# Two-layer SSD, GLA and block attention trunk: nine weight pieces split by a rounding and an adding load, mixer steps kept apart, one copy moved to ScalarE

## The chip, the cores and the metric

One core of a Trainium2 chip runs the whole program. The metric is device time in microseconds of one execution, the median of three.

## The reference, cut to what matters

A sequence of 256 tokens with 1024 channels goes through two layers and a last norm, all in float32.

```python
h = rms_norm(x, norm_w); u = h @ w_in            # first layer, w_in is 1024 x 5408
z_a, xbc, dt_raw, q_b, k_b, v_b, gate_lr, g_b = split_cols(u, EVEN_SPLITS)
y_a = rms_norm(ssd_chunked_scan(...) * silu(z_a), ssd_norm_w)          # after conv and silu of xbc
o_b = rms_norm(gla_chunked(q_b, k_b, v_b, log_decay), gla_norm_w) * silu(g_b)
x = x + concatenate([y_a, o_b]) @ w_out
h = rms_norm(x, norm_w); q, k, v, z = split(h @ w_in2)                 # second layer
x = x + (moba_attention(q, k, v) * silu(z)) @ w_out2                   # causal, one block of 256
return rms_norm(x, final_norm)
```

## The kernel before, in words

Every weight product is done in three matmuls of a rounded format (float32r): a number is split into a high part, which is its rounding, and a low part, which is what the rounding left, and `mm3` adds high by high, high by low and low by high. The weights arrive as pieces: `fetch` loads one of 128 x 1024 floats (512 KB) from SyncE's queue into one of 4 raw buffers, and `split` makes the high part on ScalarE (line 77) and the low part on VectorE (line 78), each into one of NW = 7 buffers. `plan` lists the pieces in the order of use, and `need` asks for the next few ahead of it (`prefetch`, AHEAD = 4), so that loads and splits stand in the queues before the matmuls that use them.

The first layer runs block by block in the order ORDER_A: a number j is a block of 128 columns (24 matmuls of 128 x 256, accumulated in `pb`), "a2" to "a4" are groups of 416 columns (48 matmuls, `pa`). Blocks 18 to 25 are the gate z. Then come the output products `pc1` (the GLA half) and `pc0` (the SSD half), the second layer's `pv`, `pp` and the last product `pf`.

Between those matmuls TensorE does the mixers' own small work: the SSD scan (`co_pair`: transposes `xtp`, decays `ab`, products `yp`), the GLA (`co_gla_pair`: scores `gs`, outputs `go`, transposes `obt`), the turns of `x1` into `h1` (`co_turn`: transposes `htp`, named by the token half and the column half, as `htp11`) and a few more. Each is a Python generator; every `yield` gives a delay in nanoseconds, a step is due when a planner's clock, which adds a cost for each matmul, has passed it, and `mm3` calls `due()` behind every three matmuls. All steps that are due then go out at once. TensorE's order is as written; the other engines are ordered by a scheduler when the program is built. Each engine works through its queue in order.

`part` runs one half of the tokens (tt) over eight k-blocks of three matmuls. `pv01` is the second half of the tokens in the second layer's first product: its k-blocks 4 to 7 read what `htp11` turned, rounded by ScalarE (line 741) with the low part made by VectorE (line 742).

In `co_gla_pair` the scores of two heads are copied from PSUM by ScalarE (line 604), masked by GpSimd (line 605), and a crossing block of 64 x 128 is copied over by VectorE (line 607). For each head then come two squares on ScalarE, two small VectorE steps (lines 623, 624), a power on GpSimd (line 625), one more VectorE step and the scaled output `ob`.

Of the kernel before, what the change touches and what calls it, by code (L numbers as in the profile page):

```python
# [19 lines left out]
EPS = 1e-6  # L20
# [25 lines left out]
def trunk(ctx, tc, xw_d, x_d, cst_d, mat_d, gw2_d, fn_d, wa_d, wb_d, wc_d, wv_d, wp_d, wf_d, out_d):  # L46
    nc = tc.nc
    V, S, G, TE = nc.vector, nc.scalar, nc.gpsimd, nc.tensor

    cpool = ctx.enter_context(tc.tile_pool(name="consts", bufs=1))  # L50
    wraw = ctx.enter_context(tc.tile_pool(name="wraw", bufs=4))
    whi = ctx.enter_context(tc.tile_pool(name="whi", bufs=NW))
    wlo = ctx.enter_context(tc.tile_pool(name="wlo", bufs=NW))
    big = ctx.enter_context(tc.tile_pool(name="big", bufs=1))
    tmp = ctx.enter_context(tc.tile_pool(name="tmp", bufs=2))
    sm = ctx.enter_context(tc.tile_pool(name="sm", bufs=2))
# [8 lines left out]
    def pm(name):  # L65
        return psm.tile([P, 512], F32, name=name, tag="m")


    def fetch(src, kbs, cols, name):
        raw = wraw.tile([P, kbs, cols], F32, name="r_" + name, tag="raw")  # L70
        nc.sync.dma_start(raw, src)
        return raw

    def split(raw, kbs, cols, name):
        hi = whi.tile([P, kbs, cols], F32R, name="h_" + name, tag="hi")
        lo = wlo.tile([P, kbs, cols], F32R, name="l_" + name, tag="lo")
        S.activation(hi, raw, AF.Copy)  # L77
        V.tensor_sub(lo, raw, hi.bitcast(F32))  # L78
        return hi, lo

    pieces, index, got, raws = [], {}, [], []

    def plan(key, src, kbs, cols):
        index[key] = len(pieces)
        pieces.append((key, src, kbs, cols))

    def prefetch(end):
        for j in range(len(got), min(len(pieces), end)):
            k_, src, kbs, cols = pieces[j]
            name = "_".join(str(q_) for q_ in k_)  # L90
            if j >= len(raws):
                raws.append(fetch(src, kbs, cols, name))
            got.append(split(raws[j], kbs, cols, name))
# [10 lines left out]
    for kb in range(KB):  # L104
        for c in range(2 if kb < 2 else 1):
            plan(("a01", kb, c), None, 1 if kb < 2 else 2, 416)
    for j in ORDER_A:
        if isinstance(j, str):
# [17 lines left out]

    clock = {"now": 0.0, "seq": 0}
    waiting = []  # L130

    def spend(ns):
# [2 lines left out]
    def spawn(gen, delay=0.0):  # L135
        clock["seq"] += 1
        heapq.heappush(waiting, (clock["now"] + delay, clock["seq"], gen))

    def step():
        _, _, gen = heapq.heappop(waiting)  # L140
        try:
            spawn(gen, next(gen))
        except StopIteration:
            pass

    def due():
        while waiting and waiting[0][0] <= clock["now"]:
            step()

    def drain():  # L150
        while waiting:
            clock["now"] = max(clock["now"], waiting[0][0])
            step()
# [8 lines left out]
    def tr(out, in_):  # L162
        TE.transpose(out, in_, ident)
        spend(107)
# [43 lines left out]
    tri = [mat[:, M_TRI + P * i:M_TRI + P * i + P] for i in range(2)]  # L208
    mask = mat[:, M_MASK:M_MASK + 3 * P]
    ones = cpool.tile([P, 1], F32, name="ones")  # L210
    mhalf = cpool.tile([P, 2], F32, name="mhalf")
    V.memset(ones, 1.0)
    V.memset(mhalf, -0.5)
    scanm = big.tile([P, 16, 64], F32, name="scanm", tag="s3")
# [9 lines left out]
    with tc.manual_schedule(engines={mybir.EngineType.DVE, mybir.EngineType.Activation}):  # L224
        for kb in range(KB):
# [3 lines left out]
            else:  # L229
                S.activation(hhi[:, kb, :], xk, AF.Copy, scale=en)  # L230
            V.scalar_tensor_tensor(hlo[:, kb, :], xk, en, hhi[:, kb, :].bitcast(F32),
                                   op0=ALU.mult, op1=ALU.subtract)
# [30 lines left out]
    rhalf, rsq, rsv, rsh = (cpool.tile([P, 2], F32, name=n_) for n_ in ("rhalf", "rsq", "rsv", "rsh"))  # L263
# [320 lines left out]
    def co_gla_pair(b):  # L584
        e1, e2, e3, e4, dl = env["gla"]
        qs, ks = env["qs"], env["ks"]
        rows = [slice(64 * j, 64 * j + 64) for j in range(2)]
        heads = [2 * b, 2 * b + 1]
        sps = [pm(f"gs{h}") for h in heads]
        blkv = lambda a, r, c0, n: a[r, 4 * b + c0:4 * b + c0 + n, :].rearrange("p a b -> p (a b)")  # L590
        for sp_, r in zip(sps, rows):
            mm(sp_[:, 0:P], blkv(e2, r, 0, 2), blkv(e1, r, 0, 2))
        for sp_, r in zip(sps, rows):
            mm(sp_[:, P:2 * P], ks[r, b, :, :].rearrange("p a b -> p (a b)"),
               qs[r, b, :, :].rearrange("p a b -> p (a b)"))
        for sp_, r in zip(sps, rows):
            mm(sp_[:, 2 * P:3 * P], blkv(e2, r, 2, 2), blkv(e1, r, 2, 2))
        for i in range(2):
            for sp_, r in zip(sps, rows):
                mm(sp_[0:64, 384 + 64 * i:448 + 64 * i], e4[r, 4 * b + 2 * i, :], e3[r, 4 * b + 2 * i + 1, :])  # L600
        sTs = []
        for h, sp_ in zip(heads, sps):
            sT = tmp.tile([P, 3, P], F32, name=f"sT{h}", tag="t1d")
            S.activation(sT.rearrange("p a b -> p (a b)"), sp_[:, 0:3 * P], AF.Copy)
            G.affine_select(out=sT[:, 0:3:2, :], in_=sT[:, 0:3:2, :], pattern=[[0, 2], [1, P]],
                            compare_op=ALU.is_ge, fill=0.0, base=0, channel_multiplier=-1)
            V.tensor_copy(sT[0:64, 0:3:2, 64:P], sp_[0:64, 384:512].rearrange("p (a b) -> p a b", a=2))
            sTs.append(sT)
        yield DL["gla1"]
        obs = []  # L610
        for h, sT in zip(heads, sTs):
            op = pm(f"go{h}")
            vc = slice(P * h, P * h + P)
            mm(op[:, 0:P], sT[:, 0, :], v[:, 0, vc])
            mm(op[:, P:T], sT[:, 1, :], v[:, 0, vc], True, False)
            mm(op[:, P:T], sT[:, 2, :], v[:, 1, vc], False, True)
            sq = tmp.tile([P, T], F32, name=f"osq{h}", tag="t1e")
            ss = sm.tile([P, 2], F32, name=f"oss{h}", tag="oss")
            for tt in range(2):
                S.activation(sq[:, tt * P:tt * P + P], op[:, tt * P:tt * P + P], AF.Square,  # L620
                             accum_out=ss[:, tt:tt + 1])
            rr = sm.tile([P, 2], F32, name=f"rr{h}", tag="rr")
            V.tensor_tensor(ss, ss, rsv, op=ALU.mult)
            V.tensor_scalar(ss, ss, EPS, None, op0=ALU.add)
            G.tensor_tensor(rr, ss, mhalf, op=ALU.pow)  # L625
            V.tensor_tensor(rr, rr, rsh, op=ALU.mult)
            ob = tmp.tile([P, T], F32, name=f"ob{h}", tag="t1f")
            for tt in range(2):
                V.scalar_tensor_tensor(ob[:, tt * P:tt * P + P], op[:, tt * P:tt * P + P], rr[:, tt:tt + 1],
                                       gs[:, tt, vc], op0=ALU.mult, op1=ALU.mult)  # L630
            obs.append(ob)
        yield DL["gla2"]
        obhi, oblo = env["ob"]
        gn = cst[:, C_GN:C_GN + 1]
        for h, ob in zip(heads, obs):
            tp = pm(f"obt{h}")
            for tt in range(2):
                tr(tp[:, tt * P:tt * P + P], ob[:, tt * P:tt * P + P])
            S.activation(obhi[:, h, :], tp[:, 0:T], AF.Copy, scale=gn)
            V.scalar_tensor_tensor(oblo[:, h, :], tp[:, 0:T], gn, obhi[:, h, :].bitcast(F32),  # L640
                                   op0=ALU.mult, op1=ALU.subtract)

    def co_gla():
# [6 lines left out]
    spawn(co_first(gemm_a01()))  # L650
    spawn(co_gla())
    due()
    for blk in ORDER_A:
        if isinstance(blk, str):
# [41 lines left out]
    for b in range(KB):  # L696
# [3 lines left out]
                               op0=ALU.mult, op1=ALU.subtract)  # L700
# [44 lines left out]
    r1 = cpool.tile([P, 2], F32, name="r1")  # L745
# [3 lines left out]
    def co_norm():  # L749
        s = sm.tile([P, 2], F32, name="sn", tag="sn")  # L750
        V.tensor_tensor(s, ssn[:, :, 0], ssn[:, :, 1], op=ALU.add)
        V.tensor_scalar(s, s, 1.0 / D, EPS, op0=ALU.mult, op1=ALU.add)
        G.tensor_tensor(r1, s, mhalf, op=ALU.pow)
        V.tensor_scalar(rq, r1, -0.125, None, op0=ALU.mult)
        env["r1"] = True
        yield DL["rb1"]
        S.activation(rb1, row_bcast([r1[:, tt:tt + 1] for tt in range(2)], "rb1p")[:, 0:T], AF.Copy)
# [89 lines left out]
    for g in range(4):  # L847
        qks = []
        for pr in (2 * g, 2 * g + 1):
            qk = []  # L850
            for i in range(2):
# [3 lines left out]
                hi = big.tile([P, n_], F32R, name=f"qkh{pr}_{i}", tag=(("cbT0", "cbT1"), ("qs", "ks"))[i][pr % 2])  # L855
                lo = big.tile([P, n_], F32R, name=f"qkl{pr}_{i}", tag=(("s3", "s4"), ("bc", "gs"))[i][pr % 2])
# [159 lines left out]
```

## Time and profile before

| | us |
|---|---|
| median of 3 runs | 340.42 |
| lowest and highest | 338.98, 341.65 |
| the profiled execution | 340.22 |
| its span, first to last instruction | 338.5 |

The profile is of one execution. PE is TensorE's matmuls, PEld its weight loads, DVE is VectorE, ACT ScalarE, POOL GpSimd, SP SyncE. A row of the timeline has the start, the duration and the operation with out<-in; matmuls overlap, so the distance from start to start tells the pace and not the duration. In brackets stands the idle time of the engine ahead of the row and what ended it.

### The profile page before, as it was taken

How to read it: one execution, taken by the hardware profiler on the slowest of the kernel's cores; microseconds unless marked ns; L12 is line 12 of the kernel's file. 1: busy time of each engine (PE TensorE's matmuls, PEld its weight loads, DVE VectorE, ACT ScalarE, POOL GpSimd, SP SyncE). 2: the span in 40 equal slices, each digit the busy share in tenths (PEclk: the TensorE clock that was granted, in tenths of full speed). 3: DMA queues.
4: the chain of work that ended last, by engine and by line, in shares of the span. 5: the costliest groups of instructions: out<-in, count | busy, mean ns of one | idle time of the engine just before them, and what ended most of it. 6: DMA issues, size and time to landing. Idle time of an engine off the chain costs nothing.

```text
span 338.5 us, 5905 instructions
## 1 busy us (share of the span) xinstructions
PE 327.8 (97%) x2153; PEld 293.9 (87%) x2153; DVE 259.4 (77%) x543; ACT 232.7 (69%) x501; POOL 27.1 (8%) x44
## 2 busy tenths in 40 slices
PE   8999999999997999999999999999999999999992
PEld 8999999999996979999888888888888887888792
DVE  4978978999999587689964775467869699696563
ACT  6858789959868646678352676475696996969420
POOL 2010000000001211344200000000000000000010
PEclk9999999999999999999999999999999999999997
DMA  7985582575427346241685635756408146070003
GB/s 294 406 266 180 166 257 103 178 241 190 135 95 255 124 141 216 80 152 36 221 286 179 192 122 184 248 166 222 173 24 287 65 141 232 1 248 3 0 2 125
DMA packets 16254, 56.15 MB, mean 166 GB/s; under 512 B 1968, under 2 KB 2480, under 8 KB 16096
## 3 DMA queue, kind: packets, MB, share of 16 engines
q1 hardware_dynamic: 15360, 53.37, 46.6%
q10 hardware_dynamic: 864, 2.39, 2.0%
q8 instruction: 17, 0.28, 0.3%
q14 instruction: 13, 0.11, 0.1%
HBM read 54.71 MB, written 1.05 MB: 165 GB/s over the span
## 4 chain that ended last, share of the span: by engine, by line
PE 49%; DVE 20%; ACT 17%; issue 6%; DMA 4%; POOL 2%; POOLq 0%; ACTq 0%; DVEq 0%
PE pc L159 13%; PE pp L159 10%; PE pv L159 6%; PE pa L159 6%; PE pf L159 5%; DVE l_b L78 3%; PE pb L159 3%; DMA r_b<-in_wb 3%; ACT h_p L77 3%; DVE cu L467 2%; DVE l_p L78 2%; ACT pt L810 2%; ACT h_b L77 2%; ACT pt L814 2%; POOL rr L625 1%
## 5 line engine op out<-in xcount | busy, mean ns | idle before, releaser
L159 PE MATMUL pb<-hh,h_b 128*128 128x256 f32 x416 | 76.4, 285 | 0.0
L159 PE MATMUL pp<-h,h_p 128*128 128x512 f32 x192 | 67.3, 402 | 0.0
L159 PEld LDWEIGHTS pb<-hh,h_b 128*128 128x128 f32 x416 | 64.8, 191 | 0.4 <-issue 0.2
L159 PE MATMUL pb<-hh,l_b 128*128 128x256 f32 x208 | 58.8, 283 | 0.0
L159 PE MATMUL pp<-h,l_p 128*128 128x256 f32 x192 | 50.0, 281 | 0.0
L159 PE MATMUL pa<-h_a,hh 128*128 128x416 f32 x160 | 43.1, 359 | 0.0
L159 PEld LDWEIGHTS pp<-h,h_p 128*128 128x128 f32 x192 | 34.5, 188 | 6.7
L159 PEld LDWEIGHTS pb<-hh,l_b 128*128 128x128 f32 x208 | 39.8, 191 | 0.0
L159 PEld LDWEIGHTS pp<-h,l_p 128*128 128x128 f32 x192 | 36.3, 189 | 2.2
L78 DVE TENSOR_TENSOR l_p<-r_p,h_p 128x1024 fp32r<-128x1024 f32 x24 | 29.2, 1223 | 8.8 <-ACT h_p L77 8.1
L78 DVE TENSOR_TENSOR l_b<-r_b,h_b 128x1024 fp32r<-128x1024 f32 x26 | 31.5, 1216 | 2.1 <-ACT h_b L77 2.0
L77 ACT ACTIVATE h_b<-r_b 128x1024 fp32r<-128x1024 f32 x26 | 27.2, 1062 | 5.8 <-DMA r_b<-in_wb 3.0
L159 PEld LDWEIGHTS pa<-h_a,hh 128*128 128x128 f32 x160 | 30.4, 191 | 0.7 <-ACT h_a L77 0.2
L77 ACT ACTIVATE h_p<-r_p 128x1024 fp32r<-128x1024 f32 x24 | 25.2, 1058 | 1.7 <-PE pv L159 1.6
L159 PE MATMUL pa<-l_a,hh 128*128 128x416 f32 x80 | 25.0, 351 | 0.0
L78 DVE TENSOR_TENSOR l_c<-r_c,h_c 128x1024 fp32r<-128x1024 f32 x16 | 19.9, 1253 | 5.6 <-ACT h_c L77 5.6
L77 ACT ACTIVATE h_c<-r_c 128x1024 fp32r<-128x1024 f32 x16 | 16.9, 1055 | 9.6 <-DMA r_c<-in_wc 5.6
L159 PE MATMUL pv<-h_v,h 128*128 128x512 f32 x64 | 20.2, 391 | 0.0
L810 ACT ACTIVATE pt<-pt,nm 128x128 f32<-128x128 f32 (+1 forms) x32 | 14.2, 445 | 3.0 <-DVE nm L808 3.0
L467 DVE SCALAR_TENSOR_TENSOR cu<-pad,cwh,cu 128x256 f32<-128x256 f32 x30 | 14.5, 482 | 2.1 <-ACT cu L465 1.9
L159 PEld LDWEIGHTS pa<-l_a,hh 128*128 128x128 f32 x80 | 15.1, 189 | 0.2
L352 ACT ACTIVATE pp_s<-pp 128x256 f32<-128x256 f32 x24 | 8.7, 376 | 8.8 <-PE pp L159 8.8
(244 smaller groups left out, 711.8 us busy)
## 6 DMA issues: line engine op xcount, KB each, us to landing
r_b<-in_wb SPq DMA_DIRECT2D x26, 512.0 KB, 4.5
r_p<-in_wp SPq DMA_DIRECT2D x24, 512.0 KB, 4.2
r_c<-in_wc SPq DMA_DIRECT2D x16, 512.0 KB, 3.9
r_a<-in_wa SPq DMA_DIRECT2D x12, 416.0 KB, 3.5
r_v<-in_wv SPq DMA_DIRECT2D x8, 512.0 KB, 4.5
r_f<-in_wf SPq DMA_DIRECT2D x8, 512.0 KB, 4.5
xw<-in_xw SPq DMA_DIRECT2D x6, 546.0 KB, 6.5
x<-in_x ACTq DMA_DIRECT2D x1, 1024.0 KB, 7.2
```

Source lines behind the costliest of these rows:

```text
L77: S.activation(hi, raw, AF.Copy)
L78: V.tensor_sub(lo, raw, hi.bitcast(F32))
L159: TE.matmul(out, lhsT, rhs, start=start, stop=stop)
L352: S.activation(t_, ps[:, T:2 * T], AF.Copy)
L467: V.scalar_tensor_tensor(u, pd[:, 1 + i:1 + i + T], w(i), u, op0=ALU.mult, op1=ALU.add)
L625: G.tensor_tensor(rr, ss, mhalf, op=ALU.pow)
L810: S.activation(pt[:, cs], pt[:, cs], AF.Exp, scale=-1.0, bias=nm[:, tt:tt + 1], accum_out=sme[:, tt:tt + 1])
L814: S.activation(pt[:, cs], pt[:, cs], AF.Copy, scale=sme[:, tt:tt + 1])
```

## The change

Nine pieces (blocks 12, 2, 3, 13, 5, 15, 4, 16 and 6) are no longer fetched by SyncE and split by two engines. A load issued by GpSimd writes the rounded high part straight into its buffer (line 108 of the changed kernel, two pieces ahead); ScalarE writes its negative into the low buffer; a second load by GpSimd adds the piece to it from memory (line 86). `due()` now runs one step that has TensorE work and holds the others until the planner's clock has gone on by GAP = 1500 ns; `drain()`, which empties the list behind block 25, doesn't look at the hold. In `co_gla_pair` the crossing block is copied by ScalarE ahead of the mask, and the small steps of two heads are done as one, behind both heads' outputs.

```diff
--- before.py
+++ after.py
@@ -30,6 +30,7 @@
 ORDER_A = (8, 9, 10, 11, 0, 14, 1, 12, 2, "a3", 3, 13, 5, 15, 4, 16, 6, 17, 7, "a2", "a4")
+GAP = 1500
 GLA_NEEDS = ("a3", "a3", "a4", "a4")
@@ -78,6 +79,17 @@
         V.tensor_sub(lo, raw, hi.bitcast(F32))
         return hi, lo
+    def split_dma(hi, src, kbs, cols, name):
+        lo = wlo.tile([P, kbs, cols], F32R, name="l_" + name, tag="lo")
+        S.activation(lo, hi.bitcast(F32), AF.Copy, scale=-1.0)
+        G.dma_start(lo, src, accum_op=ALU.add)
+        return hi, lo
+    def by_dma(k_):
+        return k_[0] == "b" and k_[1] in (12, 2, 3, 13, 5, 15, 4, 16, 6)
+    his = {}
     pieces, index, got, raws = [], {}, [], []
     def plan(key, src, kbs, cols):
@@ -88,6 +100,16 @@
         for j in range(len(got), min(len(pieces), end)):
             k_, src, kbs, cols = pieces[j]
             name = "_".join(str(q_) for q_ in k_)
+            for i in range(j, min(len(pieces), j + 3)):
+                ki, si, kbi, ci = pieces[i]
+                if by_dma(ki) and i not in his:
+                    his[i] = whi.tile([P, kbi, ci], F32R, name="h_" + "_".join(str(q_) for q_ in ki), tag="hi")
+                    G.dma_start(his[i], si)
+            if by_dma(k_):
+                raws.append(None)
+                got.append(split_dma(his[j], src, kbs, cols, name))
+                continue
             if j >= len(raws):
                 raws.append(fetch(src, kbs, cols, name))
             got.append(split(raws[j], kbs, cols, name))
@@ -126,7 +148,7 @@
-    clock = {"now": 0.0, "seq": 0}
+    clock = {"now": 0.0, "seq": 0, "hold": 0.0}
     waiting = []
     def spend(ns):
@@ -144,8 +166,12 @@
             pass
     def due():
-        while waiting and waiting[0][0] <= clock["now"]:
+        while waiting and waiting[0][0] <= clock["now"] >= clock["hold"]:
+            t = clock["now"]
             step()
+            if clock["now"] > t:
+                clock["hold"] = clock["now"] + GAP
     def drain():
         while waiting:
@@ -208,7 +234,7 @@
     tri = [mat[:, M_TRI + P * i:M_TRI + P * i + P] for i in range(2)]
     mask = mat[:, M_MASK:M_MASK + 3 * P]
     ones = cpool.tile([P, 1], F32, name="ones")
-    mhalf = cpool.tile([P, 2], F32, name="mhalf")
+    mhalf = cpool.tile([P, 4], F32, name="mhalf")
     V.memset(ones, 1.0)
     V.memset(mhalf, -0.5)
     scanm = big.tile([P, 16, 64], F32, name="scanm", tag="s3")
@@ -602,31 +628,36 @@
         for h, sp_ in zip(heads, sps):
             sT = tmp.tile([P, 3, P], F32, name=f"sT{h}", tag="t1d")
             S.activation(sT.rearrange("p a b -> p (a b)"), sp_[:, 0:3 * P], AF.Copy)
+            S.activation(sT[0:64, 0:3:2, 64:P], sp_[0:64, 384:512].rearrange("p (a b) -> p a b", a=2), AF.Copy)
             G.affine_select(out=sT[:, 0:3:2, :], in_=sT[:, 0:3:2, :], pattern=[[0, 2], [1, P]],
                             compare_op=ALU.is_ge, fill=0.0, base=0, channel_multiplier=-1)
-            V.tensor_copy(sT[0:64, 0:3:2, 64:P], sp_[0:64, 384:512].rearrange("p (a b) -> p a b", a=2))
             sTs.append(sT)
         yield DL["gla1"]
-        obs = []
-        for h, sT in zip(heads, sTs):
+        obs, ops = [], []
+        ss = sm.tile([P, 2, 2], F32, name=f"oss{b}", tag="oss")
+        for i, (h, sT) in enumerate(zip(heads, sTs)):
             op = pm(f"go{h}")
             vc = slice(P * h, P * h + P)
             mm(op[:, 0:P], sT[:, 0, :], v[:, 0, vc])
             mm(op[:, P:T], sT[:, 1, :], v[:, 0, vc], True, False)
             mm(op[:, P:T], sT[:, 2, :], v[:, 1, vc], False, True)
             sq = tmp.tile([P, T], F32, name=f"osq{h}", tag="t1e")
-            ss = sm.tile([P, 2], F32, name=f"oss{h}", tag="oss")
             for tt in range(2):
                 S.activation(sq[:, tt * P:tt * P + P], op[:, tt * P:tt * P + P], AF.Square,
-                             accum_out=ss[:, tt:tt + 1])
-            rr = sm.tile([P, 2], F32, name=f"rr{h}", tag="rr")
-            V.tensor_tensor(ss, ss, rsv, op=ALU.mult)
-            V.tensor_scalar(ss, ss, EPS, None, op0=ALU.add)
-            G.tensor_tensor(rr, ss, mhalf, op=ALU.pow)
-            V.tensor_tensor(rr, rr, rsh, op=ALU.mult)
+                             accum_out=ss[:, i, tt:tt + 1])
+            ops.append(op)
+        rr = sm.tile([P, 2, 2], F32, name=f"rr{b}", tag="rr")
+        pair = lambda a: a[:, None, :].to_broadcast([P, 2, 2])
+        V.tensor_tensor(ss, ss, pair(rsv), op=ALU.mult)
+        V.tensor_scalar(ss, ss, EPS, None, op0=ALU.add)
+        G.tensor_tensor(rr, ss, mhalf.rearrange("p (a b) -> p a b", a=2), op=ALU.pow)
+        V.tensor_tensor(rr, rr, pair(rsh), op=ALU.mult)
+        for i, (h, op) in enumerate(zip(heads, ops)):
+            vc = slice(P * h, P * h + P)
             ob = tmp.tile([P, T], F32, name=f"ob{h}", tag="t1f")
             for tt in range(2):
-                V.scalar_tensor_tensor(ob[:, tt * P:tt * P + P], op[:, tt * P:tt * P + P], rr[:, tt:tt + 1],
+                V.scalar_tensor_tensor(ob[:, tt * P:tt * P + P], op[:, tt * P:tt * P + P], rr[:, i, tt:tt + 1],
                                        gs[:, tt, vc], op0=ALU.mult, op1=ALU.mult)
             obs.append(ob)
         yield DL["gla2"]
@@ -750,7 +781,7 @@
         s = sm.tile([P, 2], F32, name="sn", tag="sn")
         V.tensor_tensor(s, ssn[:, :, 0], ssn[:, :, 1], op=ALU.add)
         V.tensor_scalar(s, s, 1.0 / D, EPS, op0=ALU.mult, op1=ALU.add)
-        G.tensor_tensor(r1, s, mhalf, op=ALU.pow)
+        G.tensor_tensor(r1, s, mhalf[:, 0:2], op=ALU.pow)
         V.tensor_scalar(rq, r1, -0.125, None, op0=ALU.mult)
         env["r1"] = True
         yield DL["rb1"]
```

GpSimd's queue before, from the norm's power in the first layer's start to the GLA's copies (`rcol` the norm, `cbT` the SSD scores' mask, `qs` and `ks` GLA operands):

```order
L247 TENSOR_TENSOR rcol_361<-rcol_v_360,mhalf_136 128x2
L494 AFFINE_SELECT cbT0_691<-cbT0_691 128x2x128
L494 AFFINE_SELECT cbT1_697<-cbT1_697 128x2x128
L576 COPY qs_1291<-e3_1275 128x4x64
L579 COPY ks_1292<-e4_1276 128x4x64
```

and of the changed kernel, in the stretch around the same masks (`h_b_5` is the high part of block 5, `l_b_3` the low part of block 3):

```order
L108 DMA h_b_3_746<-in_wb 128x1024
L108 DMA h_b_13_801<-in_wb 128x1024
L520 AFFINE_SELECT cbT0_698<-cbT0_698 128x2x128
L520 AFFINE_SELECT cbT1_704<-cbT1_704 128x2x128
L108 DMA h_b_5_823<-in_wb 128x1024
L108 DMA h_b_15_840<-in_wb 128x1024
L86 DMA l_b_3_825<-in_wb 128x1024
L86 DMA l_b_13_842<-in_wb 128x1024
L108 DMA h_b_4_873<-in_wb 128x1024
L86 DMA l_b_5_875<-in_wb 128x1024
L108 DMA h_b_16_896<-in_wb 128x1024
L86 DMA l_b_15_898<-in_wb 128x1024
```

Eighteen loads have come into this queue, ten of them in these rows; the low part of a piece stands behind the high part of the piece two further on.

ScalarE's queue before, around the last turn `htp11` in the second layer (`h_v1_3`, `h_p_0`, `h_p_1` are high parts of weight pieces, `va` the values):

```order
L741 ACTIVATE h1_2318<-htp01_2501,cst_104 128x128 x2
L741 ACTIVATE h1_2318<-htp11_2572,cst_104 128x128
L757 ACTIVATE rb_233<-rb1p_2585 128x256
L741 ACTIVATE h1_2318<-htp11_2572,cst_104 128x128
L774 ACTIVATE va_2520<-pv00_2521,r1_2319 128x512
L741 ACTIVATE h1_2318<-htp11_2572,cst_104 128x128
L77 ACTIVATE h_v1_3_2622<-r_v1_3_2620 128x1024
L741 ACTIVATE h1_2318<-htp11_2572,cst_104 128x128
L77 ACTIVATE h_p_0_2634<-r_p_0_2632 128x1024
L77 ACTIVATE h_p_1_2646<-r_p_1_2644 128x1024
```

and now:

```order
L805 ACTIVATE va_2487<-pv00_2488,r1_2286 128x512
L788 ACTIVATE rb_233<-rb1p_2542 128x256
L78 ACTIVATE h_v1_3_2589<-r_v1_3_2587 128x1024
L772 ACTIVATE h1_2285<-htp11_2557,cst_104 128x128
L78 ACTIVATE h_p_0_2601<-r_p_0_2599 128x1024
L772 ACTIVATE h1_2285<-htp11_2557,cst_104 128x128 x2
L78 ACTIVATE h_p_1_2613<-r_p_1_2611 128x1024
L772 ACTIVATE h1_2285<-htp11_2557,cst_104 128x128
```

The roundings of `htp11` came before `h_p_0` and `h_p_1`; now they stand between them.

TensorE's order before, at the end of `pv00` and the start of `pv01`:

```order
L159 MATMUL pv00_2521<-h_v0_3_2524,h1_2318 128x512
L159 MATMUL pv00_2521<-l_v0_3_2525,h1_2318 128x512
L159 MATMUL pv00_2521<-h_v0_3_2524,h1_2318 128x512
L163 MATMUL htp11_2572<-mat_105,x1_1683 128x128 x4
L163 MATMUL rb1p_2585<-mat_105,r1_2319 128x128 x2
L159 MATMUL pv00_2521<-h_v0_3_2524,h1_2318 128x512
L159 MATMUL pv00_2521<-l_v0_3_2525,h1_2318 128x512
L159 MATMUL pv00_2521<-h_v0_3_2524,h1_2318 128x512
L159 MATMUL pv01_2593<-h_v0_0_2429,h1_2318 128x512
L159 MATMUL pv01_2593<-l_v0_0_2430,h1_2318 128x512
L159 MATMUL pv01_2593<-h_v0_0_2429,h1_2318 128x512 x2
L159 MATMUL pv01_2593<-l_v0_0_2430,h1_2318 128x512
```

and now, inside `pv01`:

```order
L185 MATMUL pv01_2547<-h_v0_0_2396,h1_2285 128x512 x2
L185 MATMUL pv01_2547<-l_v0_0_2397,h1_2285 128x512
L185 MATMUL pv01_2547<-h_v0_0_2396,h1_2285 128x512
L185 MATMUL pv01_2547<-h_v0_1_2408,h1_2285 128x512
L185 MATMUL pv01_2547<-l_v0_1_2409,h1_2285 128x512
L185 MATMUL pv01_2547<-h_v0_1_2408,h1_2285 128x512
L189 MATMUL htp11_2557<-mat_105,x1_1615 128x128 x4
L185 MATMUL pv01_2547<-h_v0_1_2408,h1_2285 128x512
L185 MATMUL pv01_2547<-l_v0_1_2409,h1_2285 128x512
L185 MATMUL pv01_2547<-h_v0_1_2408,h1_2285 128x512
L185 MATMUL pv01_2547<-h_v0_2_2420,h1_2285 128x512
L185 MATMUL pv01_2547<-l_v0_2_2421,h1_2285 128x512
```

The four transposes `htp11` stood three matmuls ahead of the end of `pv00`; now they stand nine matmuls into `pv01`, three ahead of the first that reads `h_v0_2` (the fifth k-block).

## Rows read from the trace of the kernel before

**Rows 1.** Page, part 1: busy us (share of the span) and instructions of each engine.

```profile
PE 327.8 (97%) x2153; PEld 293.9 (87%) x2153; DVE 259.4 (77%) x543; ACT 232.7 (69%) x501; POOL 27.1 (8%) x44
```

**Rows 2.** Timeline of PE, 91 to 94 us: start, us, line, operation [idle before].

```profile
91.24 0.40 PE L159 MATMUL pb<-hh,h_b 128*128 128x256 f32 x2
91.48 0.28 PE L159 MATMUL pb<-hh,l_b 128*128 128x256 f32 x1
91.69 1.52 PE L159 MATMUL yp<-e,xdt 128*64 128x256 f32 x16
93.14 0.44 PE L163 MATMUL xtp<-mat,xs 128*128 128x128 f32 x2
93.33 0.48 PE L159 MATMUL ab<-ahl,sel 128*128 128x256 f32 x2
93.65 0.39 PE L159 MATMUL pb<-hh,h_b 128*128 128x256 f32 x2
```

**Rows 3.** Timeline of PE, 107 to 125 us.

```profile
107.28 0.44 PE L163 MATMUL xtp<-mat,xs 128*128 128x128 f32 x2
108.62 0.35 PE L159 MATMUL ab<-ahl,sel 128*128 128x256 f32 x1 [0.91 <-DVE y L533]
110.00 0.38 PE L159 MATMUL ab<-ahl,sel 128*128 128x256 f32 x1 [1.02 <-DVE xdt L509]
...
123.37 0.38 PE L163 MATMUL obt<-mat,ob 128*128 128x128 f32 x2
124.53 0.41 PE L163 MATMUL obt<-mat,ob 128*128 128x128 f32 x2 [0.78 <-DVE y L533]
```

**Rows 4.** Stages: busy us (count) of PE, PEld, DVE, ACT, POOL; PEclk, DMA share, GB/s.

```profile
10.00:20.00 10.00, 10.00 (x54) 9.88 (x54) 9.84 (x19) 9.12 (x18) 0.00 (x0) 1.00 1.03 382
...
65.00:66.00 1.00, 1.00 (x11) 1.00 (x10) 1.00 (x1) 1.00 (x3) 0.00 (x0) 1.00 0.89 340
80.00:90.00 10.00, 10.00 (x86) 10.00 (x85) 10.00 (x20) 7.86 (x16) 0.53 (x1) 1.00 0.48 156
90.00:100.00 10.00, 10.00 (x71) 9.35 (x70) 10.00 (x18) 8.43 (x17) 0.40 (x1) 1.00 0.33 98
```

**Rows 5.** Groups by line, DVE and ACT: count, busy us, mean ns.

```profile
L78 DVE TENSOR_TENSOR l_b<-r_b,h_b 128x1024 fp32r<-128x1024 f32 x26 | 31.5, 1216 | 2.1 <-ACT h_b L77 2.0
...
L607 DVE COPY sT<-gs 64x128 f32<-64x128 f32 x8 | 2.3, 282 | 3.3 <-POOL sT L605 3.2
...
L77 ACT ACTIVATE h_b<-r_b 128x1024 fp32r<-128x1024 f32 x26 | 27.2, 1062 | 5.8 <-DMA r_b<-in_wb 3.0 <-PE pa L159 2.6
```

**Rows 6.** Timeline of PE, 206 to 209 us.

```profile
206.42 0.60 PE L163 MATMUL htp<-mat,x 128*128 128x128 f32 x4
...
207.00 0.48 PE L159 MATMUL pv<-h_v,h 128*128 128x512 f32 x1
...
207.54 0.63 PE L159 MATMUL pv<-h_v,h 128*128 128x512 f32 x2
...
208.24 0.63 PE L159 MATMUL pv<-h_v,h 128*128 128x512 f32 x2
```

**Rows 7.** Timeline of ACT and of DVE, 207 to 212 us.

```profile
207.06 0.37 ACT L741 ACTIVATE h<-htp,cst 128x128 fp32r<-128x128 f32 x1 [1.61 <-PE htp L163]
...
209.36 1.06 ACT L77 ACTIVATE h_v<-r_v 128x1024 fp32r<-128x1024 f32 x1 [0.30 <-PE pv L159]
...
210.45 1.23 DVE L78 TENSOR_TENSOR l_v<-r_v,h_v 128x1024 fp32r<-128x1024 f32 x1 [1.01 <-ACT h_v L77]
211.59 0.34 DVE L742 SCALAR_TENSOR_TENSOR h<-htp,cst,h 128x128 fp32r<-128x128 f32 x1
```

**Rows 8.** Loads of `r_b`: page, part 6, and the landing times of the tile.

```profile
r_b<-in_wb SPq DMA_DIRECT2D x26, 512.0 KB, 4.5
...
DMA to landing us min/median/max: 3.4/4.5/8.6
```

**Rows 9.** Timeline of POOL.

```profile
47.69 0.84 POOL L494 TENSOR_SCALAR_AFFINE_SELECT cbT<-cbT 128x256 f32<-128x256 f32 x2 [24.64 <-ACT cbT L491]
```

## The prediction

> **What bounds the kernel now.** I read the page's first part, then TensorE's timeline over the whole span, then the groups by line and the stages, and last the loads.
>
> The page puts TensorE at 97% of the span and the next engine, VectorE, at 77% [rows 1]. A busy TensorE is not yet a TensorE at its peak, so the timeline decides. There one block of 24 matmuls of 128x256 goes on at 0.24 us for two, 0.12 each: 91.24 to 91.48 [rows 2]. That is 2.88 us for a block, and the same pace is held in block after block from 24 us on. What departs from it is short. Going through all starts between 5 and 326 us I find only two places where the engine stands still for long [rows 3]. At 107.28 the two transposes of `xtp` take 1.34 us until the next start, where the same pair took 0.19 at 93.14 [rows 2, 3]; the first `ab` then takes 1.38 us, where a pair took 0.32 at 93.33. The first wait was ended by VectorE's `y` (line 533), the second by its `xdt` (line 509). At 123.37 two `obt` transposes take 1.16 us, again until VectorE's `y`. Taking the ordinary cost off: (1.34 - 0.19) + (1.38 - 0.16) + (1.16 - 0.19) = 3.4 us. Everything else between 5 and 326 us is matmuls at pace and small steps between them.
>
> Why VectorE was late is in the stages: it is busy 10.00 of 10 us from 80 to 90 and again from 90 to 100 [rows 4], just ahead of the stall. So a queue on VectorE had formed, and TensorE felt it twice. No lightening of VectorE or ScalarE can bring more than these 3.4 us, 1.0% of the time; that is the ceiling of the change.
>
> **The change part by part.** The sum is made against the profiled execution, 340.22 us (a span of 338.5), which stands 0.2 under the median of 340.42.
>
> *Work off VectorE.* Nine subtractions of 1.216 us go [rows 5]: 10.9 us, all before 90 us. Eight crossing copies of 0.282 go: 2.3 us more. Four of eight sets of small steps for the norm go as well. ScalarE loses nothing: the rounding of 1.062 us [rows 5] becomes a negation of the same 128x1024 shape, and it gets the eight copies. By 107 us VectorE has 10.9 us less behind it, over four times the 2.4 us that TensorE stood still there. So I take both stalls as gone: -3.4 us. What is late next is nothing on VectorE in this stage.
>
> *Steps kept apart.* A mixer step put between matmuls costs more than its own matmuls: after the last 128x256 at 91.48 the next start is 0.21 later, 0.09 over the pace, and after the `ab` pair at 93.33 it is 0.32, 0.08 over [rows 2]. That is 0.17 us for each visit, shared when two steps come together, as `yp` and `xtp` did here. I counted the visits in TensorE's order between blocks 8 and 25: 24 before, 30 now; and one more in the turns of `x1` behind them. Seven more at 0.17: +1.2 us, with zero as the other end if the small steps find cover.
>
> *A turn pushed late.* The gap also holds in the second half. The last turn, `htp11`, stood among the last matmuls of `pv00`; now `rb1p` comes due first, sets the hold, and `htp11` falls nine matmuls into `pv01`, three ahead of the fifth of its eight k-blocks, the first that multiplies what was turned. Before, `htp11` started at 206.42 and its first use was twelve `pv01` matmuls and a few others later. The new chain, with 0 at the start of the turns and a k-block of three matmuls taking 0.70 (207.54 to 208.24) [rows 6]:
> - The next matmul stands 0.58 behind the turns (206.42 to 207.00), so the last k-block before the use runs 0.58 to 1.28.
> - ScalarE's first rounding of the turn starts at 0.64 (206.42 to 207.06) and takes 0.37 [rows 6, 7]: in time. VectorE is in `l_v1_3` until 1.8, since ScalarE's `h_v1_3` is only released by the end of the second k-block, about -0.5 (at 209.36 the same one waited for PE `pv`) [rows 7]. Its low part comes at 2.1; TensorE's third matmul, due 1.74, waits 0.4.
> - Next in ScalarE's queue is `h_p_0`. It takes the buffer of piece `v0_1`, which this very `pv01` reads last in the k-block that ends at 1.28. So it starts about 1.5 and ends 2.6; only then comes the second rounding of the turn, at 2.8. On VectorE `l_p_0` (1.23 us, 1.14 to the next start [rows 7]) stands in front of the second low part, which is there at 4.1. TensorE ends that k-block at 4.3, where 2.7 was due.
> - The third follows within a k-block. The fourth stands behind `h_p_1` and `l_p_1` in the same way: low part at 7.2, k-block ended 7.4, where 1.28 + 4 x 0.69 = 4.0 was due.
>
> That is +3.4 us. TensorE is the bound from here to the end, so nothing gives it back. The bounds are 0 (if the two queues ran ahead by one item) and 3.6 (every 1.2 us subtraction in front counted in full, three of them).
>
> *The split by two loads.* Each of nine pieces now comes as two loads of 0.524 MB and a negation. The latency alone is covered: a load takes 4.5 us from issue to landing in the middle, 8.6 at worst [rows 8], the chain 4.5 + 1.1 + 4.5 = 10.1 us, and a rounding load can go out once the buffer seven pieces back is free, about six blocks or 17 us ahead. The adding load stands on GpSimd behind the rounding load two pieces later, and that waits for its own buffer: it goes out four blocks, 11.5 us, ahead of use. GpSimd had nothing in that stretch (idle 24.64 us before `cbT`) [rows 9], so its queue is free for it; `cbT` now stands among the loads but waits for nothing they bring.
>
> The rate is another matter. Pieces 3, 13, 5, 15, 4, 16 and 6 stand in a row: 14 loads, 7.34 MB, in 7 x 2.88 = 20.2 us, 364 GB/s. The busiest single microsecond near this place moved 340 GB/s at a DMA share of 0.89 [rows 4], the start 382 with all engines full. At 340 GB/s the 14 loads take 21.6 us: 1.4 late. The two rounding loads that go out early (3.1 us of transfer) and the two plain pieces 17 and 7 that SyncE fetches meanwhile (3.1 us) cancel. No row shows a rounding or adding load, nor what GpSimd takes to issue one. The lower end is 0 (at 382 GB/s it is 19.2 us), the upper end 9 (below). I take 1.4, next to the row for a plain load.
>
> The Trainium skill, "DMA: Bandwidth & Descriptors", section "Where 436 GB/s comes from", says that about 358 GB/s of memory bandwidth per core is what binds a load. By that figure the 14 loads take 20.5 us, 0.3 late; the trace's own 382 GB/s over ten microseconds lies above the page, so the rows are kept.
>
> Sum: 340.2 - 3.4 + 1.2 + 3.4 + 1.4 = 342.8 us.
>
> **The rivals.**
> *The adding load is the bound.* It reads its destination too. If that counts as a second stream, the seven adding loads weigh twice: 21 x 0.524 = 11.0 MB, 32.4 us at 340 GB/s, 12.2 late, some 9 with the early loads taken off. It decides as soon as the adding load costs over 1.2 of a plain one. For it: 0.89 of the DMA engines' time went into plain loads at 340 GB/s [rows 4], so they have no room. Against it: the same row is one microsecond, and the a3 stage ahead gives slack. Time: 341.4 + 9 = 350. The Trainium skill, same page, section "SDMA does more than copy", describes the add as a reduction of two streams, which speaks for this rival; no run here shows it.
>
> *Everything is covered.* The late turn finds ScalarE and VectorE an item ahead, and the loads land in time: 340.2 - 3.4 + 1.2 = 338.0, and 336.8 if the extra visits are free too. For it: VectorE waited 1.01 us ahead of `l_v` at 210.45 [rows 7], so it isn't full there. Against it: what it waited for is the very buffer release that now stands in front.
>
> *The change doesn't do what it says.* The stalls at 107 and 123 us come from the rotation of PSUM buffers, not from VectorE's load, and stay: 342.8 + 3.4 = 346.2. Against it: VectorE at 10.00 of 10 in the two stages before.
>
> **How the numbers follow.** The forecast 0.45, the adding load 0.28, covered 0.20, stalls stay 0.07. A measurement of this kernel can tell about 1% from no change, that is 337.0 to 343.8. Faster: half of the covered case, 0.10. Slower: 0.28 + 0.07 and a fifth of the forecast, 0.44. The rest, 0.46, is within 1%. The range from 337.5 to 350 leaves out the lowest part of the covered case and the upper half of the adding load's; the forecast's own is 341 to 345.
>
> **What would show it.** Right: between 105 and 125 us no start gap over 0.4 us on TensorE; 30 visits; in `pv01`, behind `htp11`, four k-blocks that take about 6 us in place of 2.8, with `h_p_0` and `h_p_1` on ScalarE between the roundings; in 60 to 85 us TensorE waits of a microsecond or two for a load of `l_b`, with DMA at 0.9. Wrong: waits there of 5 us and more (the adding load), or none anywhere and `pv01` at pace (covered), or a wait for `y` still at 107.

## The result, and the profile after

The changed kernel takes 344.5 us (median of 4 runs, 343.6 to 345.2), the kernel before 339.8 beside it (4 runs, 338.98 to 341.65): a ratio of 1.0119, with a 95% interval of 1.0087 to 1.0152. It is slower, by 4.7 us. The forecast was 342.8, the range 337.5 to 350. The profiled execution took 345.2 us with a span of 343.5, 5.0 more than the profiled one of before; it is the slowest of its four.

Where the 5.0 us lie is read from four starts on TensorE: the first `pb`, the first `pc`, the first `pv` and the first `pp`. Before:

```profile
24.47 0.40 PE L159 MATMUL pb<-hh,h_b 128*128 128x256 f32 x2
...
156.19 0.40 PE L159 MATMUL pc<-h_c,obhi 128*128 128x512 f32 x1
...
201.62 0.40 PE L159 MATMUL pv<-h_v,h 128*128 128x512 f32 x1
...
224.12 0.39 PE L159 MATMUL pp<-h,h_p 128*128 128x512 f32 x1
```

After:

```profile
24.52 0.40 PE L185 MATMUL pb<-hh,h_b 128*128 128x256 f32 x2
...
157.32 0.48 PE L185 MATMUL pc<-h_c,obhi 128*128 128x512 f32 x1
...
202.89 0.39 PE L185 MATMUL pv<-h_v,h 128*128 128x512 f32 x1
...
229.10 0.39 PE L185 MATMUL pp<-h,h_p 128*128 128x512 f32 x1
```

The first layer (`pb` to `pc`) takes 132.80 us in place of 131.72, the stage from `pv` to `pp` 26.21 in place of 22.50. The rest is equal to 0.2 us. So the change lost 3.7 us in `pv` and 1.1 net in the first layer.

The page's first part and its DMA queues (megabytes, share of 16 engines' span), to hold against [rows 1]:

```profile
PE 329.9 (96%) x2153; PEld 293.4 (85%) x2153; DVE 246.1 (72%) x514; ACT 233.9 (68%) x509; POOL 38.9 (11%) x58
...
q1 hardware_dynamic: 14064, 48.65, 41.2%
q0 software_dynamic: 2592, 9.44, 11.5%
```

VectorE is 13.3 us lighter, as meant, and the kernel is slower all the same. The q0 row is the new one: GpSimd's 18 loads are 16% of the megabytes and 21% of what the queues took of the DMA engines.

TensorE's timeline in the first layer has three holes where `pb` waits for the low part:

```profile
69.50 0.40 PE L185 MATMUL pb<-hh,h_b 128*128 128x256 f32 x2
71.05 0.38 PE L185 MATMUL pb<-hh,l_b 128*128 128x256 f32 x1 [1.15 <-DMA l_b<-in_wb]
...
73.78 0.40 PE L185 MATMUL pb<-hh,h_b 128*128 128x256 f32 x2
74.75 0.39 PE L185 MATMUL pb<-hh,l_b 128*128 128x256 f32 x1 [0.56 <-DMA l_b<-in_wb]
...
77.93 0.40 PE L185 MATMUL pb<-hh,h_b 128*128 128x256 f32 x2
79.93 0.39 PE L185 MATMUL pb<-hh,l_b 128*128 128x256 f32 x1 [1.60 <-DMA l_b<-in_wb]
```

A pair should take 0.24 [rows 2]; here it takes 1.55, 0.97 and 2.00, that is 3.8 us too much. In the same stretch the stages show DMA engines with no time left (columns as in [rows 4]):

```profile
65.00:70.00 5.00, 4.90 (x41) 4.69 (x40) 1.76 (x5) 1.44 (x3) 0.09 (x1) 1.00 1.06 247
70.00:75.00 5.00, 3.39 (x26) 3.19 (x27) 2.39 (x4) 5.00 (x9) 1.50 (x2) 1.00 1.10 305
75.00:80.00 5.00, 3.40 (x29) 3.20 (x28) 2.95 (x6) 2.61 (x5) 0.99 (x2) 1.00 1.07 223
```

The share is over 1 (packets overlap on an engine), and yet only 223 to 305 GB/s move, where 382 were moved at a share of 1.03 before [rows 4].

In `pv01` TensorE and ScalarE stand as foretold:

```profile
212.10 0.40 PE L185 MATMUL pv<-l_v,h 128*128 128x512 f32 x1
212.85 1.06 PE L185 MATMUL pv<-h_v,h 128*128 128x512 f32 x2 [0.35 <-DVE h L773]
213.75 0.40 PE L185 MATMUL pv<-l_v,h 128*128 128x512 f32 x1
214.68 0.90 PE L185 MATMUL pv<-h_v,h 128*128 128x512 f32 x2 [0.53 <-DVE h L773]
```

```profile
211.35 0.37 ACT L772 ACTIVATE h<-htp,cst 128x128 fp32r<-128x128 f32 x1
212.05 1.06 ACT L78 ACTIVATE h_p<-r_p 128x1024 fp32r<-128x1024 f32 x1 [0.33 <-PE pv L185]
213.01 0.35 ACT L772 ACTIVATE h<-htp,cst 128x128 fp32r<-128x128 f32 x1
214.66 0.37 ACT L772 ACTIVATE h<-htp,cst 128x128 fp32r<-128x128 f32 x1 [1.30 <-DVE h L773]
215.21 1.06 ACT L78 ACTIVATE h_p<-r_p 128x1024 fp32r<-128x1024 f32 x1 [0.18 <-PE pv L185]
216.18 0.35 ACT L772 ACTIVATE h<-htp,cst 128x128 fp32r<-128x128 f32 x1
```

`h_p` waits for TensorE's `pv`, and the next rounding of the turn stands behind it.

### The profile page after: what moved, and what is told of

It is laid out like the page before. It is cut to its first block, busy times and chain, and to the rows that moved or that the text cites. A ratio compares the mean times of both kernels' runs of the same rounds, so it can differ in the third digit from the quotient of the medians.

```text
span 343.5 us, 5914 instructions
## 1 busy us (share of the span) xinstructions
PE 329.9 (96%) x2153; PEld 293.4 (85%) x2153; DVE 246.1 (72%) x514; ACT 233.9 (68%) x509; POOL 38.9 (11%) x58
## 3 DMA queue, kind: packets, MB, share of 16 engines
q0 software_dynamic: 2592, 9.44, 11.5%
## 4 chain that ended last, share of the span: by engine, by line
PE 67%; ACT 10%; DVE 8%; issue 7%; DMA 4%; POOL 3%; POOLq 0%; ACTq 0%
PE pb L185 14%; PE pc L185 13%; PE pa L185 11%; PE pp L185 10%; PE pv L185 6%; PE pf L185 5%; ACT h_p L78 3%; DMA l_b<-in_wb 3%; DVE l_p L79 3%; ACT pt L841 2%; PE yp L185 2%; ACT pt L845 2%; DMA xw<-in_xw 1%; PE gs L185 1%; PE go L185 1%
## 5 line engine op out<-in xcount | busy, mean ns | idle before, releaser
L185 PE MATMUL pb<-hh,h_b 128*128 128x256 f32 x416 | 77.3, 286 | 0.0
L79 DVE TENSOR_TENSOR l_p<-r_p,h_p 128x1024 fp32r<-128x1024 f32 x24 | 29.2, 1223 | 11.5 <-ACT h_p L78 10.9
L79 DVE TENSOR_TENSOR l_c<-r_c,h_c 128x1024 fp32r<-128x1024 f32 x16 | 19.3, 1220 | 8.0 <-ACT h_c L78 7.9
L79 DVE TENSOR_TENSOR l_b<-r_b,h_b 128x1024 fp32r<-128x1024 f32 x17 | 20.6, 1221 | 4.5 <-ACT h_b L78 4.5
L185 PE MATMUL pv<-h_v,h 128*128 128x512 f32 x64 | 21.6, 405 | 2.0 <-DVE h L773 1.4
L78 ACT ACTIVATE h_b<-r_b 128x1024 fp32r<-128x1024 f32 x17 | 17.9, 1060 | 2.4 <-PE pb L185 1.6
L185 PEld LDWEIGHTS pv<-h_v,h 128*128 128x128 f32 x64 | 11.9, 188 | 6.8 <-DVE h L773 3.0
```

The lines of the kernel that those rows point to most:

```text
L185: TE.matmul(out, lhsT, rhs, start=start, stop=stop)
```

## The experiments

Eleven kernels, each timed against the kernel before on its own chip: behind the time stand the ratio to it and its 95% interval. The kernel before had medians of 339.54 to 340.42 us on these chips, so differences between kernels from different chips are uncertain by up to 0.9 us. "Gap" is the distance from one start to the next on TensorE.

**No split by loads.** The changed kernel with

```diff
-        return k_[0] == "b" and k_[1] in (12, 2, 3, 13, 5, 15, 4, 16, 6)
+        return False
```

> The changed kernel with all pieces fetched and split as before; the hold of 1500 ns and the ScalarE crossing block stay. Theory (late adding loads cost about 4.2 us of the 4.7 that were lost, the late turn about 3.4, the stalls at 107 and 123 us were VectorE's load and are spared by the hold and the crossing block too): 344.5 - 4.2 = 340.3 us, start gaps of 1 us and more between 60 and 85 us gone, pv01 still 3.4 us late. Rival 1 (the nine subtractions off VectorE are what removed the stalls): the stalls of 3.4 us come back, 343.7 us. Rival 2 (the loads only made TensorE wait where it would have waited for something else): no gain, 344 to 345 us.

Measured: 341.1 us, 1.0040 (1.0026 to 1.0053). The loads cost 3.4 us by the medians; the first layers differ by 4.3 (132.80 and 128.48). No wait of TensorE over 0.1 us is left between 24 and 207 us, and no gap over 0.3 at 105 to 125 us, so the stalls of [rows 3] stay away although all 26 subtractions are back on VectorE. The rival that these subtractions were what mattered falls.

**The hold in the first layer alone.** The changed kernel with

```diff
-                clock["hold"] = clock["now"] + GAP
+                clock["hold"] = clock["now"] + clock["gap"]
...
     drain()
+    clock["gap"] = 0
```

(`clock["gap"]` begins as GAP.)

> The changed kernel with the hold set to 0 once the list is emptied behind block 25, so that it acts in the first layer alone and the turn htp11 is back among the last matmuls of pv00. Theory (the pushed turn costs 3.4 us): 344.5 - 3.4 = 341.1 us, pv01's eight k-blocks at 0.7 us each. Rival (ScalarE and VectorE have the same items to do before the next product, so the wait only moves behind pv01): 344 to 345 us, with waits at pp0 or in the k-blocks of pv10.

Measured: 340.42 us, 1.0025 (1.0009 to 1.0041). The pushed turn costs 4.1 us by the medians; `pv` to `pp` takes 22.49 us again, and no wait shows up behind it.

**Both edits.**

> Both of the two edits: no split by loads, hold in the first layer alone; what is left of the change is the hold ahead of block 25 and the crossing block with the joint norm steps on ScalarE. Theory (the two losses are independent): 344.5 - 4.2 - 3.4 = 336.9 us, under the kernel before by the stalls of 3.4 us less some extra visits. Rival 1 (subtractions were what freed VectorE): 340.3 us, with TensorE standing still at 105 to 125 us. Rival 2 (the losses cover for each other): 339 to 341 us without such stalls.

Measured: 337.32 us, 0.9924 (0.9907 to 0.9941), faster than both kernels. The two losses are independent: 344.5 - 3.4 - 4.1 = 337.0. The first layer takes 128.66 us, 3.06 less than before. The stalls were worth 3.34, so the six further visits in it cost 0.3 us.

**The ScalarE block alone.** The same without hold (`GAP = 0`) and without the split.

> The kernel before with the crossing block on ScalarE and the joint norm steps alone; no hold (0 ns), no split by loads. Theory (VectorE's load ahead of 107 us makes the stalls; 8 copies of 0.282 us are 2.3 us, of which about half lie ahead of 107 us): the stalls shrink by 1 to 2 us, 338 to 339 us. Rival 1 (the stall comes from steps that come due together, which only the hold parts): no change, 339.8 us. Rival 2 (all relief needed is there): 336.4 us.

Measured: 339.22 us, 0.9974 (0.9958 to 0.9989). The pieces of the stall are now 0.9, 0.2 and 0.7 us in place of 1.15, 1.22 and 0.97, which is the theory's size; the median lies 0.2 us over its range. The second one nearly went: there `ab` waits for a small PSUM buffer, before for the one that VectorE's `xdt` frees [rows 3], and `xdt` stood behind `l_b`. By the semaphores in this trace it now waits for ScalarE, which alone reads the scores and their crossing block and frees their buffer sooner.

**The subtractions left out.** The kernel before with

```diff
     def split(raw, kbs, cols, name):
+        if name in ("b_12", "b_2", "b_3", "b_13", "b_5", "b_15", "b_4", "b_16", "b_6"):
+            hi = whi.tile([P, kbs, cols], F32R, name="h_" + name, tag="hi")
+            S.activation(hi, raw, AF.Copy)
+            return hi, hi
```

> The kernel before, with the nine subtractions on VectorE left out: the nine pieces have no low part of their own, the high part stands in its place in the products. Everything else, loads and order, as before. Theory of the prediction (10.9 us less on VectorE remove the stalls at 107 and 123 us by themselves): 339.8 - 3.4 = 336.4 us, no start gap over 0.4 us between 105 and 125 us. Rival (the queue that delays y forms behind 90 us, or the steps that come due together make it): the stalls stay, 339 to 340 us.

Measured: 339.25 us, 0.9983 (0.996 to 1.0006), no difference that can be told. TensorE at the two places:

```profile
108.34 0.44 PE L167 MATMUL xtp<-mat,xs 128*128 128x128 f32 x2
108.54 0.36 PE L163 MATMUL ab<-ahl,sel 128*128 128x256 f32 x1
109.65 0.39 PE L163 MATMUL ab<-ahl,sel 128*128 128x256 f32 x1 [0.74 <-DVE xdt L513]
...
123.02 0.38 PE L167 MATMUL obt<-mat,ob 128*128 128x128 f32 x2
124.17 0.41 PE L167 MATMUL obt<-mat,ob 128*128 128x128 f32 x2 [0.77 <-DVE y L537]
```

The wait behind `xtp` is gone (0.20). The one between the two `ab` is still 1.11, and the one at `obt` 1.15. With 10.9 us less on VectorE, 1.9 of the 3.34 us stay (pieces of 0.95 and 0.96, with the ordinary cost off).

**The adding load made a plain one.** The second kernel above with

```diff
-        G.dma_start(lo, src, accum_op=ALU.add)
+        G.dma_start(lo, src)
```

> The kernel with the hold in the first layer alone (340.4 us), with the adding load replaced by a plain load of the same piece into the same buffer on the same queue, behind the same negation: the low part is then the whole piece and not what the rounding left. Theory (an adding load occupies the DMA engines for nearly twice a plain one's time, and the engines are full from 55 to 85 us): most of the 3.1 us come back, 337.3 to 338.5 us, the share of q0 falls from 11.5% to about 8%, and l_b lands in 5 to 6.5 us. Rival 1 (the row of two loads and a negation is too long for seven buffers, whatever the load does): 340.4 us, waits for l_b as before. Rival 2 (seven plain loads more are too many at 340 GB/s, 1.4 us, as predicted): 338.7 us.

Measured: 337.39 us, 0.9928 (0.9903 to 0.9954): all of the loss is back, with the same bytes on the same queue in the same order. Its stage, its q0 and its loads:

```profile
65.00:70.00 5.00, 5.00 (x45) 5.00 (x44) 2.05 (x5) 4.11 (x9) 0.53 (x1) 1.00 1.13 415
...
q0 software_dynamic: 2592, 9.44, 8.5%
...
h_b<-in_wb POOLq DMA_DIRECT2D x9, 512.0 KB, 5.0
l_b<-in_wb POOLq DMA_DIRECT2D x9, 512.0 KB, 5.0
```

The same two rows of the changed kernel:

```profile
h_b<-in_wb POOLq DMA_DIRECT2D x9, 512.0 KB, 6.1
l_b<-in_wb POOLq DMA_DIRECT2D x9, 512.0 KB, 8.9
```

18 plain loads take 8.5% of 336.4 us, 1.59 us each with all engines. With nine adding ones they take 11.5% of 343.5, so an adding load takes (39.5 - 9 x 1.59) / 9 = 2.8 us, 1.76 of a plain one, if the nine rounding loads take the same in both. The packets in the traces say it without that condition: of the 2304 packets of 4 KB on this queue, 2014 take 150 to 200 ns with plain loads; in the changed kernel 1042 do, and 1054 take 300 to 350. With plain loads the same stage moves 415 GB/s, no wait for a load is left, and the chain of two loads is in time: rival 1 falls, and so does the 1.4 us that the prediction gave to the rate.

**Five pieces by loads in place of nine.** The list is (12, 3, 5, 4, 6), in the same kernel.

> The kernel with the hold in the first layer alone (340.4 us), with five pieces by two loads in place of nine: 12, 3, 5, 4 and 6, so that every second piece of the row comes by SyncE. Theory (DMA engines full): the demand of the row falls from 14 loads to 10, of which four are adding; the DMA share stays under 1 and the waits for l_b shrink to 0 to 0.7 us: 337.3 to 338 us. Rival (the chain of two loads is late for each such piece): 4 of 7 waits stay, about 339 us.

Measured: 337.56 us, 0.9932 (0.9907 to 0.9958). No TensorE wait for a load is left; the DMA share is 1.06, 0.85 and 0.91 in the three stages from 65 to 80 us, the first above the theory's 1. Five adding loads fit, nine do not; but five gain nothing either over the kernel with both edits (337.32), which has none.

**A hold of 800 ns.** In the kernel with both edits, `GAP = 800`.

> The kernel without the split by loads and with the hold in the first layer alone (337.3 us), with a hold of 800 ns in place of 1500. Theory (a further visit costs about 0.05 us and it is the parting of steps that removes the stalls; a hold of a quarter block parts most of them): 337 to 337.5 us. Rival 1 (visits cost 0.17 each, and fewer are made): 336.5 to 337 us. Rival 2 (the shorter hold lets VectorE fall behind again): a part of the 1.9 us comes back, 338 to 339 us.

Measured: 337.46 us, 0.9935 (0.991 to 0.9959): the same as with 1500. It can't tell what a visit costs, since its trace has 30 visits as well.

**The hold alone.** The kernel before with the new `due()`, in the first layer only.

> The kernel before with the hold of 1500 ns ahead of block 25 alone: no split by loads, crossing copies and norm steps as before. Theory (the stalls come from steps of several mixers that come due together and take more small PSUM buffers than there are, so that TensorE stands behind VectorE's evacuations; parting the steps is enough): stalls gone, 336.5 to 337.5 us, like the kernel that has the ScalarE block too (337.3). Rival (VectorE must be lightened as well): a part of the stalls stays, 338 to 339 us.

Measured: 338.9 us, 0.9955 (0.9935 to 0.9975). Between 105 and 125 us the largest gap is 0.29: the hold alone removes the whole of [rows 3]. But a new stall stands where the list is emptied:

```profile
151.67 0.28 PE L164 MATMUL pb<-hh,l_b 128*128 128x256 f32 x1
153.39 0.33 PE L168 MATMUL obt<-mat,ob 128*128 128x128 f32 x1 [1.44 <-DVE ob L634]
```

The last `ob` waits there for the norm steps of its head on VectorE and GpSimd. With the joint steps and the ScalarE copy (the kernel with both edits) that gap is 0.36. So neither theory is whole: the hold clears the old stalls, and the ScalarE block pays for the one that the hold makes.

**The split by loads alone.** The kernel before with `split_dma`, `by_dma` and the early rounding loads.

> The kernel before with the split of nine pieces by two loads alone: no hold, crossing copies and norm steps as before. Theory (the adding loads cost 3.1 to 3.4 us, or 4.1 in a profiled execution; without the subtractions the part of the stalls at 107.3 us goes that waits for y, 1.2 us, and the other two parts stay): 341.5 to 343 us. Rival 1 (the waits for loads give VectorE time, so all stalls go): 339.5 to 340 us. Rival 2 (the loads are late only where the hold lets TensorE run ahead): 339 us or less.

Measured: 344.6 us, 1.0121 (1.0088 to 1.0154), above what the theory gave. One wait for `l_b` takes 2.58 us (another, at 87.4, 0.29), and then the granted clock falls:

```profile
63.28 0.40 PE L179 MATMUL pb<-hh,h_b 128*128 128x256 f32 x2
66.26 0.39 PE L179 MATMUL pb<-hh,l_b 128*128 128x256 f32 x1 [2.58 <-DMA l_b<-in_wb]
...
64.00:66.00 2.00, 0.00 (x0) 0.00 (x0) 1.85 (x3) 1.20 (x2) 0.47 (x1) 1.00 1.10 320
66.00:68.00 2.00, 1.74 (x13) 1.74 (x14) 0.19 (x1) 0.64 (x1) 0.00 (x0) 0.89 1.09 238
68.00:70.00 2.00, 2.00 (x11) 2.00 (x11) 0.00 (x0) 2.00 (x4) 0.86 (x1) 0.50 1.07 211
70.00:72.00 2.00, 2.00 (x15) 2.00 (x15) 0.95 (x3) 1.06 (x2) 0.00 (x0) 0.76 1.05 295
```

At clocks of 0.89, 0.50 and 0.76 the last three stretches lose 1.7 of their 6 us, by estimate; the theory had no term for that. The wait for `y` behind `xtp` at 112 us is gone, as it said, and the other two pieces stay. One is the second `ab`, with its releaser named:

```profile
113.83 0.38 PE L179 MATMUL ab<-ahl,sel 128*128 128x256 f32 x1 [1.27 <-DVE sT L627]
```

That is the crossing copy, which frees the score's PSUM buffer; here it stands ahead of `xdt` on VectorE.

**Two `ab` in one PSUM buffer.** The kernel before with

```diff
-                ab = pm(f"ab{h}")
-                mm(ab[:, 0:T], sel[:, h:h + 1].to_broadcast([P, P]), ahl)
+                if j == 0:
+                    ab2 = pm(f"ab{h}")
+                ab = ab2[:, T * j:T * j + T]
+                mm(ab, sel[:, h:h + 1].to_broadcast([P, P]), ahl)
```

> The kernel before with the two decays ab of a block in one small PSUM buffer in place of two, all else as before. In the visit at 105 us yp, two gs, xtp and two ab take six of four buffers; now five. Theory (the buffers' rotation makes the stall): the second ab no longer waits for a score buffer, so the gap of 1.38 us at 108.62 falls to 0.3 or less, while the first ab still waits for y; 338.3 us, or 339 where the stall at 123 us moves. Rival (VectorE's load makes the stall, whatever the buffers): gaps as before, 339.6 us.

Measured: 349.26 us, 1.0271 (1.0232 to 1.0309). Neither: the second `ab` now waits until ScalarE has read the first half of the buffer, 1.2 to 2.0 us at each of eight visits, as here:

```profile
108.75 0.36 PE L159 MATMUL ab<-ahl,sel 128*128 128x256 f32 x1
110.54 0.38 PE L159 MATMUL ab<-ahl,sel 128*128 128x256 f32 x1 [1.43 <-ACT e L520]
```

It brings a wait of its own and says nothing on the question.

## Why the prediction was right, and where not

The time fell into the range and into the forecast's own, 1.7 us above its point. Term by term, in the profiled executions:

| term | predicted | measured | by |
|---|---|---|---|
| the two stalls | -3.4 | -3.3 | no gap over 0.29 at 105 to 125 us |
| further visits | +1.2 | +0.3 | both edits, against before |
| the late turn | +3.4 | +3.7 | `pv` to `pp` |
| the loads | +1.4 | +4.3 | first layer, against no split |

Together +5.0 on 340.2, where 345.2 was profiled. That the total came so near is in part luck: the loads were put 2.9 us too low, the visits 0.9 too high. By medians the loads cost 3.1 (second kernel against both edits) to 3.4, the turn 3.8 to 4.1.

*What bounds it.* Right. Only what TensorE stood still for could be won: the best kernel gains 2.5 us of the 3.4.

*The late turn.* Right in place, mechanism and size, with the order of ScalarE's queue and TensorE's k-blocks as worked out from rows 6 and 7. Two more waits, of 0.53 each, follow those shown, at 216.58 and 217.84; the last low part is there 7.1 us behind the start of the turn, where 7.2 was foretold.

*The stalls.* The number came out right by luck, and its reason failed: "By 107 us VectorE has 10.9 us less behind it, over four times the 2.4 us that TensorE stood still there. So I take both stalls as gone." Without these subtractions 1.9 of the 3.34 us stay and the time is that of before; with them and the hold the stalls go. VectorE was full from 80 to 100 us, but no queue from there reached the stall: it stood idle for 0.81 us just ahead of it. VectorE before:

```profile
106.20 0.96 DVE L521 TENSOR_TENSOR e<-e,cbT 128x768 f32<-128x768 f32 x1 [0.81 <-ACT e L520]
...
107.61 0.87 DVE L533 SCALAR_TENSOR_TENSOR y<-xs,cst,yp 128x256 f32<-128x256 f32 x2
108.39 1.22 DVE L78 TENSOR_TENSOR l_b<-r_b,h_b 128x1024 fp32r<-128x1024 f32 x1
109.53 0.42 DVE L509 TENSOR_TENSOR xdt<-xtp,dt 128x256 f32<-128x256 f32 x1
...
122.37 1.23 DVE L78 TENSOR_TENSOR l_b<-r_b,h_b 128x1024 fp32r<-128x1024 f32 x1
123.51 0.87 DVE L533 SCALAR_TENSOR_TENSOR y<-xs,cst,yp 128x256 f32<-128x256 f32 x2
```

What TensorE waited for was a small PSUM buffer: in the visit at 105 us `yp`, two `gs`, `xtp` and two `ab` ask for six of four, so the first `ab` wants one that `y` has yet to free, the second one that `xdt` has; at 123 us the second `obt` wants one that `y` has. What made `xdt`, and `y` at 123 us, late is a subtraction `l_b` just ahead of each. Neither is one of the nine: both still stand there with the nine left out. Parting the visit into three gives `y` and `xdt` the time. The rival that named the buffers had the cause and drew the wrong end from it, since it left the hold out. The releasers and the kernels with hold, copy or subtractions alone show this; a kernel with more buffers wasn't tried, nor one with these two subtractions elsewhere.

*The visits.* Over-sized at least fourfold. With the hold alone the first layer takes 130.11 us, 1.61 less than before; with 3.34 of stalls gone and 1.60 of a new one, 0.1 is left for the six visits (30 in place of 24, as counted), and 0.3 by the kernel with both edits. The 0.17 that one visit lost at 91 us is not lost again in full when a visit is parted.

*The loads.* The term that was mis-sized. "At 340 GB/s the 14 loads take 21.6 us: 1.4 late" took an adding load for a plain one, and a busy microsecond for the ceiling. Both were wrong, in opposite ways: plain loads reach 415 GB/s in the five microseconds from 65 us, and an adding one weighs 1.76. The rival "the adding load is the bound" had the mechanism, and its price of 9 was too high for the same reason. An estimate with both rows: seven plain and seven adding loads weigh 7 + 7 x 1.76 = 19.3 plain ones, 10.1 MB, at 415 GB/s 24.4 us, 4.2 later than the 20.2 that the row has. That is close to the 4.3 of the profiled executions and above the 3.1 to 3.4 of the medians; it leaves out what goes early and what SyncE fetches beside. The latency that was held to be covered was lost in the same way: the three late low parts were issued at 59.50, 63.20 and 69.91, that is 10.2, 10.8 and 8.3 us ahead of their use, not far from the 11.5 that was foretold, and took 10.0 to 11.5 us to land in place of 4.5. The Trainium skill, "DMA: Bandwidth & Descriptors", section "SDMA does more than copy", calls the add a reduction of two streams; the runs agree that it is no copy: it took 1.76 of a plain load, a little under the two that the rival reckoned with.

## What to carry to other kernels

Work taken off an engine is worth what the waiting engine's releaser says, not what the busy share says: find the buffer that is waited for, count how many of its kind the visit asks for, and look at what stands just ahead of the instruction that frees it. Moving arithmetic into an adding DMA is paid in DMA time, some 1.8 of a plain load, so it belongs only where the stage's DMA share leaves room, as five of these nine pieces show; here even these five gained nothing. A rule that spaces out work should end where its reason ends: the same hold gained in the first layer and lost all of it on one turn in the second.

## What was not expected of the hardware

- An adding load of 512 KB lands in 8.9 us in the middle and makes the rounding loads beside it slower too (6.1 us); plain loads on the same queue land in 5.0.
- 415 GB/s over five microseconds, at a DMA share of 1.13, with loads from two queues.
- In the kernel with the split alone, after a gap of 2.98 us at 63.28, the granted clock fell to 0.50 in the stretch from 68 to 70 us, the lower of its two levels (1.2 GHz), when TensorE had been at work again since 66.26; it was back at 1.00 from 72 us. In the changed kernel gaps of up to 2.00 us left it at 1.00.
- A matmul into the second half of a PSUM buffer waited for ScalarE's reading of the first half. The trace names a semaphore of ScalarE as what ended the wait, so the built program asks for it; whether the chip would have waited without it wasn't tried.
